# Two layers of a hybrid mixer with feed-forward sublayers: the last feed-forward sublayer partly by seven products instead of eight

## The chip, the cores and the metric

The kernel runs on one core of one Trainium2 chip. The metric is the device time of one execution in microseconds (us). The profile is one execution recorded by the hardware profiler. Its names for the engines: PE is TensorE (the matmuls), PEld TensorE's weight loads, DVE is VectorE, ACT is ScalarE, POOL is GpSimd and SP is SyncE, whose queue issues the DMAs.

## The reference, cut to what matters

Two layers run over 512 tokens of width 1024 and 256 context tokens. Each layer has a feed-forward sublayer, a mixer and a second feed-forward sublayer. In the last layer the second feed-forward sublayer is needed for the 512 tokens alone, and it ends the program.

```python
def swiglu(h, wg, wu, wd):
    return (jax.nn.silu(h @ wg) * (h @ wu)) @ wd
...
        x = residual(x, 0.5 * swiglu(sublayer_in(x, m_l, 2), ffn_w_gate[l, 1], ffn_w_up[l, 1], ffn_w_down[l, 1]),
                     m_l, 2, norm_g[l, 2], norm_b[l, 2])
```

`wg` and `wu` are 1024 x 2816, `wd` is 2816 x 1024, all in float32.

## The kernel before

Every float32 operand of a product is held as two float16 pieces, a rounded one and its remainder, and a product is made of three passes (large x large, large x small, small x large). `split_weight` (L319) makes the pieces of a weight: ScalarE scales and rounds (L320), VectorE subtracts (L321). Activations are split in the same way (L457, L458).

The 2816 columns of the feed-forward sublayer are 11 pairs of 256 columns, and the pairs form five groups (`GROUPS`, L355: 0-1, 2-3, 4-5, 6-7, 8-10). For each pair, gate and up are computed, the silu and the product follow, and `put_act` (L441) makes the activation's pieces. After each group its down product is added to the accumulator `acc`. The last group's down (`down_last`, L803) ends in the normalisation.

Both products can be made in two ways.

- Plain. `gate_up_plain` (L557) makes 96 products of 512 columns a pair in the 512-token sublayer (L571), in the PSUM tiles `big`. `down_plain` (L762) makes 96 products for a group of two (L772), in the PSUM tiles `sm`. A pair's gate and up need 8 weight pieces (`ring` blocks), a pair's down 4.
- By seven. A block product of 2 x 2 halves is made of seven products instead of eight (Winograd's form of Strassen's scheme). `gate_up` (L488) splits the tokens and the 1024 inputs into halves, so that a pair takes 168 products, each over half of the tokens (L511), in the PSUM tiles `pf` (one running chain for each of gate and up) and `big`; ScalarE copies the chain at three points (L518), and VectorE adds (L534, L544, L546). `down_blocks` (L722) makes the seven products of a group (L743), two token tiles at a time, in `pf` and `big`, and VectorE adds them to the accumulator (L749). The weights need sums of their quarters, which GpSimd makes (L426 to L429 for gate and up, L394 to L397 for down), and 7 pieces for each of gate, up and down. The activations need four more sums (L449 to L452) and 7 pieces instead of 4. The inputs need four differences (`tt`, made by `differences`, L463) over the whole sublayer: `input_differences` (L478) loads the scaled inputs `inp` that the sublayer before wrote to memory (L299 to L301, only where `keep` is set) and forms them on VectorE and GpSimd.

In the three sublayers of 768 tokens (`has_ctx`), pair 0 is plain, the other ten go by seven, and so do the downs of the first four groups. In the last sublayer (`whole_plain`) all pairs and groups are plain, and the inputs' differences are not made.

Weights come in loads of 1 MB into two `raw` tiles. `jobs` lists the loads and splits in the order of use, and `prepare` (L838) runs three of them ahead; the pieces stand in 21 ring blocks, five of which lie in the sublayer's own memory and can be written only after the mixer's memory is free. The differences and the copies of the chain share the tiles `pt` with the rows that the residual loads (L796). The accumulator shares the tiles `xa` with the loaded inputs. The order of the instructions on each engine is set by the tile framework's scheduler, which mixes instructions of different steps by priority and by its own estimate of time.

Of the kernel before, what the change touches and what calls it, by code (L numbers as in the profile page):

```python
# [23 lines left out]
DEPTH = 2  # L24
FF = 2816
NPAIR = FF // 256
# [17 lines left out]
def kernel(  # L44
# [25 lines left out]
    class Tags:  # L70


        def __init__(self, pool, **bufs):
            self.pool, self.bufs = pool, bufs
# [124 lines left out]
    def affine_cols(l, i, prev):  # L199

        cols = small.tile([P, 2, KC, 2], F32, tag="abc", name=f"abc{l}{i}", bufs=2)
        sc1 = small.tile([P, KC, 2], F32, tag="sc1", name=f"sc1{l}{i}", bufs=2)
        V.tensor_scalar(out=sc1, in0=mT[l][:, 3 * i + 1], scalar1=1.0, scalar2=SA, op0=ALU.add, op1=ALU.mult)
        g = gb_cols[:, 0, prev, :].unsqueeze(2).to_broadcast([P, KC, 2])
        b = gb_cols[:, 1, prev, :].unsqueeze(2).to_broadcast([P, KC, 2])
        V.tensor_tensor(out=cols[:, 0], in0=sc1, in1=g, op=ALU.mult)
        V.tensor_tensor(out=sc1, in0=sc1, in1=b, op=ALU.mult)
        V.scalar_tensor_tensor(out=cols[:, 1], in0=mT[l][:, 3 * i], scalar=SA, in1=sc1,
                               op0=ALU.mult, op1=ALU.add)
        return cols  # L210
# [25 lines left out]
    def bcast_row(src, nm, alloc):  # L236
        t = alloc([P, D], nm)
        nc.sync.dma_start(out=t, in_=src.partition_broadcast(P))
        return t
# [10 lines left out]
    class Norm:  # L250


        def __init__(self, l, i, nxt, last, arow, ayh, au32):
            self.l, self.i, self.last, self.ayh, self.au32 = l, i, last, ayh, au32
            self.st = {}
            n = 3 * l + i
            rows = (norm_g[l, i], norm_b[l, i]) if last else (agb[n], agb[6 + n])
            self.g, self.b = (bcast_row(q, f"{nm}{l}{i}", arow) for q, nm in zip(rows, ("gbc", "bbc")))
            if not last:
                self.uT = new_uT(f"uT{l}{i}")  # L260
                self.cols = affine_cols(nxt[0], nxt[1], 3 * l + i)
                self.stream = Stream((l, i))
                self.keep = nxt[1] != 1 and nxt != (DEPTH - 1, 2)

        def one(self, t, rt):

# [42 lines left out]
    def new_uT(nm):  # L309
        return main.tile([P, 2, KC, T], F16, tag="uT", name=nm, bufs=1)  # L310
# [44 lines left out]
    GROUPS = [[0, 1], [2, 3], [4, 5], [6, 7], [8, 9, 10]]  # L355

    def ffn(l, i, uT, stream, ntiles, nxt, last, todo):
        has_ctx = ntiles > NLT
# [4 lines left out]
        with tc.tile_pool(name=f"ffn{l}{i}", bufs=1) as fp:  # L363
# [14 lines left out]
                return block(shape, nm)  # L378


            whole_plain = not has_ctx
            gu_plain = set(range(NPAIR)) if whole_plain else {0}
            plain = set(range(NPAIR)) if whole_plain else set(GROUPS[-1])

            def prep_down(pr_):
                raw = load_raw(ffn_w_down[l, w, pr_ * 256:(pr_ + 1) * 256, :].rearrange("(k p) f -> p k f", p=P),
# [20 lines left out]
            def load_plain(pr_):  # L407
                for q in range(2):
                    load(pr_, q)
# [64 lines left out]
            def new_differences():  # L474
                for n in range(1, 5):
                    tt[n] = ft("T", [P, 2, 4, half], f"T{n}{l}{i}", F16)

            def input_differences():  # L478
                new_differences()
                for t in range(ntiles // 2):  # L480
                    u = []
                    for q in range(2):
                        u.append(ft("xa", [P, KC, P], f"u{l}{i}{t}{q}"))
                        nc.sync.dma_start(out=u[q], in_=stream.inputs[t + q * ntiles // 2])
                    differences(u[0][:, 0:4], u[1][:, 0:4], u[0][:, 4:8], u[1][:, 4:8], slice(0, 4),
                                slice(t * P, (t + 1) * P), [P, 4, P], f"{t}")
# [231 lines left out]
            def new_acc():  # L718
                for t in range(ntiles):
                    acc[t] = ft("xa", [P, D], f"acc{l}{i}_{t}")  # L720
# [123 lines left out]
            if start:  # L844
                finish = first_pair()
            else:
                load_plain(0)
                if not whole_plain:
                    input_differences()
            prepare(FIT)  # L850
            for gi, prs in enumerate(GROUPS):
                for q in prs:
                    if todo and (q > 1 or len(todo) >= NPAIR - 1 - q):
                        ada_vec(*todo.pop(0), al("ada"))
                    if start and q == 0:
                        finish()
                    else:
                        (gate_up_plain if q in gu_plain else gate_up)(q)
                    if q == 0:
                        new_acc()  # L860
                    ahead[0] -= 2 if q > 0 else 0
                    prepare(FIT)
                    if gi == len(GROUPS) - 1 and q < NPAIR - 1:
                        residual(q - prs[0])
                if gi < len(GROUPS) - 1:
                    (down_plain if whole_plain else down_blocks)(gi, prs)
                    ahead[0] -= 2
                    prepare(FIT)
            norm = down_last(GROUPS[-1])
# [765 lines left out]
    for n, (l, i) in enumerate(steps):  # L1635
        last = n == len(steps) - 1
        nxt = None if last else steps[n + 1]
# [70 lines left out]
```

## Time and profile before

| | |
|---|---|
| time, median of 3 runs | 2877.5 us (2873.37 to 2879.3) |
| profiled execution | 2878.8 us |
| its span | 2877.0 us |
| TensorE busy | 2656.4 us, 92% |
| VectorE busy | 2118.9 us, 74% |
| ScalarE busy | 1210.6 us, 42% |
| GpSimd busy | 1160.1 us, 40% |
| mean granted clock of TensorE | 0.973 |

The last sublayer's first product starts at 2511.95 us and its last one ends at 2868.06 us. Times in the rows are counted from the span's start. In a row of the timeline, the start and the length come first, then engine, line, operation, tiles and shapes; xN is the number of instructions merged, and the brackets give the idle time of the engine before it and what ended that. Instructions overlap in the pipeline, so the pitch of a run of N products is the difference of two starts divided by N.

### The profile page before, as it was taken

What the parts mean: (1) busy time and instruction counts of PE and PEld (TensorE: products, weight loads), DVE (VectorE), ACT (ScalarE), POOL (GpSimd) and SP (SyncE); (2) the same over time, 40 slices, a digit from 0 to 9 for tenths busy, and PEclk for the clock granted to TensorE, in tenths of its full rate; (3) what the DMA queues carried; (4) which work ended last, traced back from release to release, by engine and by line L of the source; (5) the groups of instructions that cost most, each with busy time, mean ns of one, the idle gap of its engine ahead of it and who ended that gap; (6) DMA issues with size and microseconds to landing.
All of it is one profiled execution on the core that took longest, in us unless ns stands there. A gap on an engine that the chain in (4) does not pass through costs nothing. (4 is left out here: it accounts for less than half of the span.)

```text
span 2877.0 us, 42905 instructions
## 1 busy us (share of the span) xinstructions
PE 2656.4 (92%) x16415; PEld 1554.0 (54%) x16415; DVE 2118.9 (74%) x3134; ACT 1210.6 (42%) x2619; POOL 1160.1 (40%) x1016
## 2 busy tenths in 40 slices
PE   6899999989899988999999889988999899899998
PEld 4454555557677863544555444544555667744443
DVE  4967788786867688768877988879787768634455
ACT  3443344434436444533443344433433537333321
POOL 1744465241525455534552655446242425400011
PEclk8999999999999999999999999999999999999999
DMA  7635432333234244444453422221422333152330
GB/s 242 196 127 176 133 132 98 107 121 90 78 88 105 74 176 163 160 161 147 147 169 121 165 65 82 74 66 61 156 83 87 103 107 100 67 176 88 120 122 30
DMA packets 220355, 342.63 MB, mean 119 GB/s; under 512 B 16008, under 2 KB 162166, under 8 KB 220150
## 3 DMA queue, kind: packets, MB, share of 16 engines
q1 hardware_dynamic: 220150, 339.90, 36.6%
q8 instruction: 129, 2.11, 0.3%
q14 instruction: 76, 0.62, 0.1%
HBM read 301.43 MB, written 23.22 MB: 113 GB/s over the span
## 5 line engine op out<-in xcount | busy, mean ns | idle before, releaser
L511 PEld LDWEIGHTS <-pcgu 128*128 128x128 f16 x3792 | 373.4, 99 | 329.1 <-issue 93.3
L511 PE MATMUL ch<-T,pcgu 128*128 128x384 f16 x1920 | 337.0, 329 | 5.2 <-ACT U L518 5.2
L743 PEld LDWEIGHTS <-act 128*128 128x128 f16 x1512 | 142.9, 98 | 216.4 <-issue 58.4
L321 DVE SCALAR_TENSOR_TENSOR pcgu<-rawgu,pcgu 128x512 f16<-128x512 f32 x218 | 216.3, 1008 | 49.2 <-ACT pcgu L320 48.2
L571 PE MATMUL pl<-uT,pcgu 128*128 128x512 f16 (+2 forms) x1068 | 228.0, 367 | 7.7 <-DVE uT L214 7.0
L320 ACT ACTIVATE pcgu<-rawgu 128x512 f16<-128x512 f32 x218 | 133.9, 626 | 211.5 <-PE ds L743 126.6
L429 POOL TENSOR_TENSOR S4gu<-rawgu,S2gu 128x512 f32<-128x512 f32 x60 | 90.1, 1502 | 273.7 <-DVE pcgu L321 137.3
L571 PEld LDWEIGHTS <-pcgu 128*128 128x128 f16 x1236 | 121.8, 101 | 138.5 <-issue 24.7
L511 PEld LDWEIGHTS <-pegu 128*128 128x128 f16 x1248 | 122.2, 98 | 108.2 <-issue 29.7
L800 POOL TENSOR_TENSOR acc<-acc,gate 128x512 f32<-128x512 f32 x44 | 62.2, 1421 | 282.9 <-DVE acc L780 253.7
L743 PE MATMUL ds<-pcd,act 128*128 128x512 f16 x612 | 152.3, 381 | 4.3 <-DVE acc L749 2.8
L743 PE MATMUL dc<-pcd,act 128*128 128x512 f16 x576 | 149.1, 384 | 7.2 <-DVE acc L749 7.1
L976 PEld LDWEIGHTS <-uT 128*128 128x128 f16 x1344 | 134.7, 101 | 29.9 <-issue 8.4
L228 ACT ACTIVATE u<-pt,abc 128x128 f32<-128x128 f32 x224 | 81.2, 467 | 161.2 <-PE pt L225 98.9
L816 PE MATMUL pd<-pcd,act 128*128 128x512 f16 x594 | 141.1, 379 | 4.2 <-DVE dt L822 4.2
L321 DVE SCALAR_TENSOR_TENSOR pcd<-rawd,pcd 128x512 f16<-128x512 f32 x124 | 109.0, 893 | 40.6 <-ACT pcd L320 40.5
L426 POOL TENSOR_TENSOR S1gu<-rawgu 128x512 f32<-128x512 f32 x60 | 88.8, 1480 | 116.2 <-DMA rawgu<-in_ffn_w_gate_dram 55.8
L816 PEld LDWEIGHTS <-act 128*128 128x128 f16 x792 | 77.4, 98 | 99.2 <-issue 10.7
L458 DVE TENSOR_TENSOR act<-sg,act 128x384 f16<-128x384 f32 (+1 forms) x149 | 123.6, 873 | 3.3 <-ACT act L457 3.3
L94 POOL TENSOR_SCALAR rs<-mv 128x1 f32<-128x1 f32 x32 | 17.9, 559 | 263.3 <-DVE mv L273 263.3
L518 ACT COPY U<-ch 128x384 f32<-128x384 f32 x180 | 83.6, 472 | 76.8 <-PE ch L511 76.1
L428 POOL TENSOR_TENSOR S3gu<-rawgu 128x512 f32<-128x512 f32 x60 | 96.4, 1607 | 32.4 <-DVE pegu L321 16.2
(391 smaller groups left out, 6209.5 us busy)
## 6 DMA issues: line engine op xcount, KB each, us to landing
adaw<-in_ada_w_dram SPq DMA_DIRECT2D x128, 512.0 KB
rawd<-in_ffn_w_down_dram SPq DMA_DIRECT2D x44, 1024.0 KB
rawgu<-in_ffn_w_gate_dram SPq DMA_DIRECT2D x43, 1024.0 KB
rawgu<-in_ffn_w_up_dram SPq DMA_DIRECT2D x43, 1024.0 KB
row<-yh SPq DMA_DIRECT2D x56, 256.0 KB
rawwo<-in_w_out_dram SPq DMA_DIRECT2D x8, 1024.0 KB
xt<-row SPq DMA_DIRECT2D x32, 256.0 KB
gate<-grow SPq DMA_DIRECT2D x28, 256.0 KB
```

The lines of the kernel that those rows point to most:

```text
L320: A.activation(pc[:, 0], src, AF.Copy, scale=SW)
L321: V.scalar_tensor_tensor(out=pc[:, 1], in0=src, scalar=SW, in1=pc[:, 0], op0=ALU.mult, op1=ALU.subtract)
L426: G.tensor_tensor(out=s1, in0=a21, in1=a22, op=ALU.add)
L428: G.tensor_tensor(out=s3, in0=a11, in1=a21, op=ALU.subtract)
L429: G.tensor_tensor(out=s4, in0=a12, in1=s2, op=ALU.subtract)
L458: V.tensor_tensor(out=pc[:, 1], in0=src, in1=pc[:, 0], op=ALU.subtract)
L511: PE.matmul(pp, lhsT=wt[pr_][q][m][:, a, k, :], rhs=rhs, start=(n == 0 and m in (1, 2, 5)), stop=(n == 11), skip_group_check=m in (1, 6, 7 ...
L518: A.copy(t_, chain[q])
L571: PE.matmul(pp[:, j, o:o + hi - lo], lhsT=wp.at(a, k, cc * P, (cc + 1) * P), rhs=uT[:, b, k, lo:hi], start=(n == 0), stop=(n == KC * 3 - 1))
L743: PE.matmul(pd, lhsT=acts[q][m][:, a, ts], rhs=wd[q][m][:, b], start=(n == 0 and m in (1, 2, 5)), stop=(n == len(prs) * 3 - 1), skip_group ...
L816: PE.matmul(pd, lhsT=acts[q][2 * cc + hf][:, a, o:o + P], rhs=wd[q][2 * cc + h][:, b], start=(n == 0), stop=(n == len(prs) * 6 - 1))
L976: PE.matmul(pp, lhsT=uT[:, a, k, t * P:(t + 1) * P], rhs=pc.at(b, k, 0, n_), start=(n == 0), stop=(n == KC * 3 - 1))
```

## The change

In the last sublayer the gate and up of the odd pairs (1, 3, 5, 7, 9) go by seven products, and so do the downs of groups 1 and 3 (pairs 2, 3 and 6, 7). The even pairs and the groups 0, 2 and 4 stay plain. The mixer of the last layer now writes the scaled inputs to memory (`keep`), and the sublayer loads them and forms their differences after pair 0. The 768-token sublayers stay as they are.

```diff
-                self.keep = nxt[1] != 1 and nxt != (DEPTH - 1, 2)
+                self.keep = nxt[1] != 1
...
-            whole_plain = not has_ctx
-            gu_plain = set(range(NPAIR)) if whole_plain else {0}
-            plain = set(range(NPAIR)) if whole_plain else set(GROUPS[-1])
+            gu_plain = {0} if has_ctx else set(range(0, NPAIR, 2))
+            plain = set(GROUPS[-1] + ([] if has_ctx else GROUPS[0] + GROUPS[2]))
...
                 load_plain(0)
-                if not whole_plain:
+                if has_ctx:
                     input_differences()
...
                     if q == 0:
+                        if not has_ctx:
+                            input_differences()
                         new_acc()
...
-                    (down_plain if whole_plain else down_blocks)(gi, prs)
+                    (down_plain if prs[0] in plain else down_blocks)(gi, prs)
```

## Rows read from the trace of the kernel before

**Rows 1.** The page: busy time, share of the span and instructions of each engine, and the lines of the chain that ended last.

```profile
PE 2656.4 (92%) x16415; PEld 1554.0 (54%) x16415; DVE 2118.9 (74%) x3134; ACT 1210.6 (42%) x2619; POOL 1160.1 (40%) x1016
...
PE pl L571 7%; PE pd L772 3%; PE pd L816 1%; DMA rawd<-in_ffn_w_down_dram 0%; DMA rawgu<-in_ffn_w_gate_dram 0%; DVE pcgu L321 0%; POOL yh L306 0%; POOL yh L305 0%; DMA row<-yh 0%; ACT pcd L320 0%; POOL rs L94 0%; DVE bst L271 0%; DVE pegu L321 0%; ACT L437 0%; DVE yh L286 0%
```

**Rows 2.** Busy time of each engine in two stretches of the last sublayer: start, end and length, busy us and instructions of each engine, TensorE's granted clock, the DMA engines' share and GB/s.

```profile
2529.00:2546.70 17.70, 16.04 (x144) 11.03 (x145) 6.98 (x11) 6.90 (x12) 0.00 (x0) 0.84 0.95 340
2546.70:2868.10 321.40, 321.32 (x1488) 145.44 (x1487) 147.39 (x243) 96.49 (x185) 16.48 (x14) 1.00 0.30 98
```

**Rows 3.** Who TensorE waited for from 2546.7 to 2868.1 us (us in total, times, longest).

```profile
PE pl L571 <- DVE sg L438: 1.5, 1, 1.5
```

**Rows 4.** Timeline of TensorE at the start of pair 1, products of 512 columns.

```profile
2546.72 1.46 PE L571 MATMUL pl<-uT,pegu 128*128 128x512 f16 x6 [1.51 <-DVE sg L438]
2548.01 4.05 PE L571 MATMUL pl<-uT,pcgu 128*128 128x512 f16 x18
2551.90 1.46 PE L571 MATMUL pl<-uT,pegu 128*128 128x512 f16 x6
```

**Rows 5.** Timeline of TensorE in the last mixer's output projection, products of 256 columns.

```profile
2458.19 18.61 PE L1566 MATMUL pm<-pcwo,mT 128*128 128x256 f16 x169
2476.64 1.04 PE L225 MATMUL pt<-mats,yh 128*128 128x128 f32 x8
```

**Rows 6.** Groups of instructions from 2546.7 to 2868 us (count, then busy us and mean ns of one, then idle time before them and what ended it).

```profile
L571 PEld LDWEIGHTS <-pcgu 128*128 128x128 f16 x732 | 71.6, 98 | 86.4
...
L321 DVE SCALAR_TENSOR_TENSOR pcgu<-rawgu,pcgu 128x512 f16<-128x512 f32 x55 | 38.0, 708 | 20.7 <-ACT pcgu L320 20.4
...
L458 DVE TENSOR_TENSOR act<-sg,act 128x256 f16<-128x256 f32 x44 | 16.6, 420 | 3.3 <-ACT act L457 3.3
```

**Rows 7.** Timeline of VectorE near 2543 us: three weight subtractions, and three activation pieces.

```profile
2543.12 1.89 DVE L321 SCALAR_TENSOR_TENSOR pcd<-rawd,pcd 128x512 f16<-128x512 f32 x3
...
2548.80 1.10 DVE L458 TENSOR_TENSOR act<-sg,act 128x256 f16<-128x256 f32 x3 [0.47 <-ACT act L457]
```

**Rows 8.** The line of GpSimd's first weight sum, over the whole span: durations in ns (least, median, most), first and last start.

```profile
L426 POOL TENSOR_TENSOR S1gu<-rawgu x60: 1262/1598/1721, 58.5 to 2035.2; 128x512 f32<-128x512 f32 x60
```

**Rows 9.** Timeline of SP's queue at the start of the last sublayer.

```profile
2508.77 17.71 SPq L307 DMA_DIRECT2D row<-yh  x4
2528.42 0.32 SPq L786 DMA_DIRECT2D gate<-grow  x1
2528.80 1.37 SPq L796 DMA_DIRECT2D xt<-row  x3
2530.21 0.43 SPq L337 DMA_DIRECT2D rawgu<-in_ffn_w_up_dram  x1
```

**Rows 10.** Timeline of all engines at the start of the 768-token sublayer after the first mixer: the loads of the inputs, and the first and last instruction of the differences on VectorE.

```profile
1057.38 3.57 SPq L484 DMA_DIRECT2D u<-inp  x6
...
1063.47 0.69 DVE L466 TENSOR_TENSOR t<-u,u 128x512 f32<-128x512 f32 x1 [3.51 <-DMA u<-inp]
...
1084.48 1.28 DVE L472 TENSOR_TENSOR T<-t,T 128x512 f16<-128x512 f32 x2
```

**Rows 11.** Timeline of TensorE in pair 1 of the same sublayer, the rows with a wait.

```profile
1079.30 1.46 PE L511 MATMUL ch<-uT,pegu 128*128 128x384 f16 x8 [1.36 <-DVE sg L438]
...
1086.41 2.11 PE L511 MATMUL sd<-uT,pegu 128*128 128x384 f16 x12 [1.70 <-ACT sg L437]
...
1093.56 1.12 PE L511 MATMUL ch<-uT,pcgu 128*128 128x384 f16 x3 [4.71 <-DVE sg L438]
...
1107.15 1.35 PE L511 MATMUL sd<-T,pegu 128*128 128x384 f16 x6 [3.99 <-DVE sg L534]
```

**Rows 12.** Timeline of TensorE in pair 1 of the second layer's 768-token sublayer, the rows with the three long waits.

```profile
1651.83 2.11 PE L511 MATMUL sd<-uT,pegu 128*128 128x384 f16 x12 [3.04 <-ACT sg L437]
...
1658.98 4.00 PE L511 MATMUL ch<-uT,pcgu 128*128 128x384 f16 x12 [3.74 <-DVE sg L438]
...
1672.54 4.00 PE L511 MATMUL sd<-T,pegu 128*128 128x384 f16 x12 [3.57 <-DVE sg L534]
```

**Rows 13.** Busy time of each engine in one cycle of two pairs and a down of the same sublayer, and in 4.2 us of it (columns as in rows 2).

```profile
1785.80:1878.56 92.76, 84.75 (x463) 45.49 (x463) 75.72 (x96) 39.11 (x74) 45.03 (x33) 0.98 0.22 69
1825.00:1829.20 4.20, 3.60 (x12) 1.66 (x12) 2.42 (x4) 1.62 (x4) 2.73 (x3) 0.62 0.01 3
```

**Rows 14.** Who TensorE waited for in that cycle, the four largest (us in total, times, longest).

```profile
PE dc L743 <- DVE acc L749: 3.1, 2, 2.8
PE ch L511 <- DVE acc L749: 2.8, 1, 2.8
PE sd L511 <- DVE up L534: 0.8, 1, 0.8
PE ch L511 <- ACT U L518: 0.6, 1, 0.6
```

**Rows 15.** Timeline of TensorE in that cycle: 12 products after a wait, and 12 without one.

```profile
1825.10 3.60 PE L511 MATMUL ch<-uT,pcgu 128*128 128x384 f16 x12 [2.83 <-DVE acc L749]
...
1832.83 2.11 PE L511 MATMUL sd<-T,pcgu 128*128 128x384 f16 x12
```

**Rows 16.** Groups of instructions in that cycle (columns as in rows 6): the largest group of weight subtractions, and of activation pieces.

```profile
L321 DVE SCALAR_TENSOR_TENSOR pcgu<-rawgu,pcgu 128x512 f16<-128x512 f32 x9 | 10.5, 1176 | 1.0 <-ACT pcgu L320 1.0
L458 DVE TENSOR_TENSOR act<-sg,act 128x384 f16<-128x384 f32 x7 | 9.8, 1448 | 0.0
```

## The prediction

> **What bounds the kernel now.** The page first: TensorE is busy 92% of the span, and the chain that ended last names L571, the gate/up products of the plain pairs, more than any other line [rows 1]. Then the busy time by stretches: from 2546.7 to 2868.1 us, the last sublayer after its first pair, TensorE is busy 321.3 of 321.4 us at full granted clock, VectorE 147 us and GpSimd 16 us [rows 2]. The list of waits has one entry there, 1.5 us at its start [rows 3]. So each TensorE microsecond saved there is one of the time, until another engine takes its place, and each wait that the change brings costs at once.
>
> **What a product costs.** 24 products of 512 columns start from 2546.72 to 2551.90: 215.8 ns each [rows 4]. For 256 columns, which the change uses, the nearest rows are the mixer's output products, 169 with a new weight each from 2458.19 to 2476.64: 109.2 ns [rows 5]. A weight load takes 98 ns [rows 6] and fits beside. Against this stands the Trainium skill, "TensorE: Matmul & The Clock Gate", section "Back-to-back issue gap": a sustained stream of loads and products at about 81 ns for 128 columns and 131 ns for 512. By an estimate between these, 98 ns for 256 columns, seven products would cost a pair 16.4 us against 12.6, so 3.8 us more. The 215.8 ns measured at 512 differ from the page, and the rows decide.
>
> **What goes.** Gate/up of a pair: 2 matrices x 2 column halves x 8 k x 3 passes = 96 products x 215.8 ns = 20.72 us. By seven: 7 x 2 matrices x 4 k x 3 passes = 168 of 256 columns x 109.2 ns = 18.35 us. Saved 2.37 us, in five pairs (1, 3, 5, 7, 9) 11.9 us. Down of a group of two: 96 products become 7 x 2 tiles x 2 pairs x 3 = 84, still of 512 columns: 12 x 215.8 ns = 2.59 us, in two groups (pairs 2, 3 and 6, 7) 5.2 us. Together **17.1 us**, all on the path.
>
> **What comes on the other engines.** Seven products need 14 weight pieces for 8 (five pairs) and 7 for 4 (four down matrices): 30 + 12 = 42 more splits, each a ScalarE scale and a VectorE subtraction. Three of these take 1.89 us, one 0.69, so they issue every 0.60 us; activation pieces (three in 1.10, one 0.42) every 0.34 [rows 7, 6]. 42 x 0.60 = 25 us. GpSimd makes 5 x 8 + 4 x 4 = 56 weight sums, of which one takes 1.26 us at least and 1.60 in the median [rows 8]: 71 to 90 us, and 16 smaller sums of activations. There are 12 more activation pieces and 28 accumulator additions instead of 16. Over 321 us no engine is full: VectorE goes from 147 to some 200 us. So I cost them at nothing, hidden by TensorE; the cover is gone where they bunch, and that is a rival below.
>
> The four writes of the scaled inputs (512 KB each) enter SP's queue at the mixer's end, among row writes and weight loads; SP stands in row writes from 2508.8 to 2526.5 anyway [rows 9], so zero. The loads of the residual's rows, issued as early as 2528.8 now [rows 9], come later, because the differences and copies take their buffers (pt); the last group needs them, with two pairs' products over them: zero, about 2 us if one were met bare. Two of the four accumulator tiles wait until the inputs' tiles are released, and are first written after pair 1: zero.
>
> **The first pairs.** By its third product pair 1 now needs the differences. Their loads can start when the mixer's memory is free, about 2528.4 us, as the next loads do now [rows 9]; the DMA engines are 95% busy from 2529 to 2546.7 [rows 2], but the residual's rows leave room. After the first mixer, 768 tokens, the same loads are issued at 1057.4, the first difference starts at 1063.5 and the last ends at 1085.8 [rows 10]: 6.1 us, then 22.3 us for three column tiles, so about 15 for two: ready near 2549.5. TensorE reaches them at about 2545.2 + 48 x 109.2 ns = 2550.4. Just in time. Yet in both 768-token sublayers TensorE stalls in pair 1, with ScalarE and VectorE, in order, busy with differences and splits: 11.8 us in four waits after the first mixer [rows 11], 10.4 in the second layer (3.0, 3.7, 3.6), and there two runs of 12 products took 4.00 us, not 2.11 [rows 12]. The 4.7 and 3.7 are for the PSUM of the 256 context tokens, not used here, and the 1.5 us of [rows 3] falls away, because pair 1 can begin in another PSUM tile. Bounds: -1.5 us, and 14 ([rows 12] with the slow products). I take 5: a wait of 3.6 us, which both have, about 2 for the silu, 1 for the clock, less 1.5.
>
> **The other pairs.** The nearest rows are a cycle of two pairs and a down in the second layer's 768-token sublayer, 92.8 us [rows 13]; the second pair of the group has only the 0.8 us for an addition out of PSUM [rows 14], the first one up to 2.8. Pairs 3, 5, 7, 9 stand second or inside a group; 256 columns leave a third less slack than 384. So 0 to 2.8 us each; I take 0.8, four times: 3.1.
>
> **The groups by seven.** Now the down's PSUM tiles (sm) are its own, and the next pair's gate/up fills every wait. By seven it takes pf and big, which that pair needs too. In the cycle of [rows 14] the down waits 3.1 us (2.8 at once) for accumulator additions, queued on VectorE behind activation pieces, which queue behind GpSimd's sums. The pair after it waited 2.8 us for pf and ran 12 products in 3.60 us, not 2.11 [rows 15], at a granted clock of 0.62 [rows 13], so partly at 1.2 GHz; here a plain pair follows, which takes big, released earlier. From 0 to 7.3 us a group (all of [rows 14]); I take 3.1 twice: 6.2.
>
> **Sum.** -17.1 + 5 + 3.1 + 6.2 = **-2.8 us**. The profiled execution took 2878.8 us, 1.8 more than its span of 2877.0, and is 1.3 above the median of 2877.5. Against the median I forecast **2874.5 us**, a saving mostly paid back, with a range of its own of 2867 to 2882.
>
> **Rivals.** (1) *Covered.* The waits are filled: pairs 0.4, groups 1.0, the start 0: -17.1 + 1.6 + 2 = -13.5, **2864**. For it: VectorE is under half busy now, and second pairs have few waits. Against: the down of the cycle waited [rows 14].
>
> (2) *VectorE full in groups 1 and 3*, the slower side. In one of them (plain pair, seven pair, down by seven: TensorE 20.7 + 18.4 + 18.1 = 57.2 us) VectorE has 36 splits, 14 activation pieces, 14 accumulator additions of 0.60 us and about 4.5 us more. Alone, 36 x 0.60 + 14 x 0.34 + 12.9 = 39 us. But with GpSimd at work the largest groups of splits and pieces take 1.18 and 1.45 us in the mean [rows 16], against 0.71 and 0.42 in the last sublayer now [rows 6]; VectorE is busy 75.7 of 92.8 us there [rows 13]. It decides once splits average over 0.96 us (pieces at 0.7, an estimate between 0.42 and 1.45): 36 x 0.96 + 9.8 + 12.9 = 57.3. At 1.18 it is 65.2, 8 over, twice 16 in place of the 6.2: -17.1 + 16 + 5 + 1.6 (pairs 5, 9) = +5.5, and with half the group waits on top +8.6: **2886**. Against it: 13 of the 36 splits may slip into the plain group that follows. The Trainium skill, "SBUF — State Buffer", section "Who interferes with whom", says that a VectorE instruction with two SBUF inputs and a GpSimd one that reads SBUF exclude each other for their whole length. The rows agree in kind; an estimate by that rule locks 36 x 0.60 + 14 x 0.34 + 16 x 1.26 + 8 x (0.65 to 1.26) = 52 to 57 of the 57 us: just full, no more.
>
> (3) *A late start.* The upper bound of the first pairs, 14 for 5: **2883.5**. The order on ScalarE and GpSimd decides.
>
> (4) *Short products not at half.* If weight loads set the pace and a 256-column product takes 123 ns, the pairs gain nothing: -2.8 + 11.9, **2886.5**. 169 products at 109.2 ns speak against it. The page cited first points that way.
>
> **Chances.** Forecast 0.48, covered 0.22, VectorE full 0.17, late start 0.09, short products 0.04. A measurement here can tell about 0.2%, 5.8 us, from no change: faster is below 2871.7, slower above 2883.3. The forecast's own range gives 0.15 faster, 0.29 same, 0.04 slower; covered is faster; the late start 0.05 same, 0.04 slower; VectorE full slower; short products 0.01 same, 0.03 slower. Faster 0.37, same 0.35, slower 0.28. From 2862 to 2888 leaves out a quarter of covered and half of VectorE full, some 0.15.
>
> **What would show it.** Right: 840 L511 products of 256 columns at 109 ns and 168 of L743 in this sublayer, TensorE's busy time there down by 17 us, and some 14 us of waits: at pair 1, and two near 3 us for L749. Covered: hardly a wait after 2560. VectorE full: its share over 95% from pair 2 to the end of group 1, splits over 1 us. Late start: waits on L471 or L472. The forecast is wrong if the groups' waits are elsewhere, or if the end's sequence changes.

## The result, and the profile after

The changed kernel takes 2900.9 us (median of 4 runs, 2897.0 to 2908.8), the kernel before beside it 2875.4 (2869.6 to 2879.3): a ratio of 1.0094, 95% interval 1.0065 to 1.0123. It is 25 us slower. The forecast was 2874.5, its range 2862 to 2888.

The profiled execution has a span of 2896.9 us. The last sublayer's first product starts at 2508.1 us, where it was 2511.95 before. From there to the end of the span it is 388.8 us against 365.05: **+23.7 us**. So nearly all of the loss lies in the changed sublayer, and this measure is given for every run below, because the work ahead of the sublayer, which the edits leave as it is but for the four writes of the inputs, varies by some microseconds from one execution to the next: in the fourteen profiled executions the first product starts between 2503.4 and 2516.1 us.

The page after, the lines that answer to [rows 1]:

```profile
PE 2641.0 (91%) x16751; PEld 1583.0 (55%) x16751; DVE 2234.2 (77%) x3247; ACT 1254.6 (43%) x2716; POOL 1268.3 (44%) x1092
...
PE pl L570 3%; PE pd L771 1%; PE pd L815 1%; DVE pcgu L321 1%; PE ch L510 1%; DVE pcd L321 1%; DVE act L457 1%; PE sd L510 1%; PE dc L742 1%; DMA rawgu<-in_ffn_w_up_dram 0%; DMA rawgu<-in_ffn_w_gate_dram 0%; DVE ped L321 0%; DVE T L471 0%; 
```

In the changed kernel the lines of the sublayer stand one lower: L510 is the product of `gate_up`, L570 of `gate_up_plain`, L742 of `down_blocks`, L748 its addition to the accumulator, L437 the product behind the silu, L457 the activation's pieces. TensorE's busy time fell by 15.4 us, as wanted, and the time rose: the chain that ended last now runs through VectorE's splits (L321) and pieces (L457) as well.

Timeline of TensorE in pair 5, of the changed kernel (answers to [rows 5]):

```profile
2683.77 2.78 PE L510 MATMUL ch<-uT,pcgu 128*128 128x256 f16 x24
2686.39 1.47 PE L510 MATMUL sd<-uT,pegu 128*128 128x256 f16 x12
2687.70 1.47 PE L510 MATMUL sd<-uT,pcgu 128*128 128x256 f16 x12
```

24 products in 2.62 us: 109.2 ns each, the price that the prediction took, and no gap. Pairs 5 and 9 lose nothing.

Busy time of each engine in stretches of the changed kernel (columns as in [rows 2]): pair 2, plain; pair 3 and the down of group 1, both by seven; pair 4 and pair 5 with 12 products of the next down between; and the first 4.9 us after the longest wait of that down.

```profile
2593.50:2614.20 20.70, 20.70 (x98) 9.35 (x97) 12.60 (x14) 10.94 (x20) 7.22 (x5) 1.00 0.28 101
2614.20:2663.10 48.90, 38.76 (x250) 24.74 (x249) 46.35 (x65) 25.10 (x53) 25.29 (x20) 0.93 0.32 104
2663.10:2706.00 42.90, 42.90 (x284) 27.53 (x283) 26.24 (x41) 19.80 (x39) 8.08 (x6) 1.00 0.40 128
...
2648.00:2652.90 4.90, 4.84 (x13) 1.72 (x13) 3.90 (x9) 0.93 (x3) 1.15 (x1) 0.57 0.20 67
```

The second row is the loss. Its products are worth 168 x 109.2 ns + 84 x 215.8 ns = 36.5 us, and it takes 48.9: 12.4 us are lost in group 1. VectorE is busy 46.35 of the 48.9 us, 95%, and that is 10 us more than the products last, so TensorE can't run ahead of it. In the row before, VectorE has 8 us idle. Pair 7 with the down of group 3 takes 52.6 us (2743.55 to 2796.18): 16.1 us are lost there. The last row shows what follows a wait: the granted clock is 0.57 of full speed, so mostly at the lower level of 1.2 GHz, and the 12 products that start from 2648.06 to 2652.69 take 4.63 us instead of 2.59.

Who TensorE waited for from 2540 to 2900 us in the changed kernel, the five largest entries (answers to [rows 3], where 1.5 us stood):

```profile
PE dc L742 <- DVE acc L748: 11.8, 2, 6.5
PE sd L510 <- DVE sg L533: 6.1, 2, 3.3
PE sd L510 <- DVE sg L437: 4.6, 3, 2.2
PE ch L510 <- DVE pcgu L321: 1.8, 2, 1.4
PE pl L570 <- DVE sg L543: 1.6, 1, 1.6
```

All five name VectorE. The 11.8 us are one wait in each down by seven (5.2 and 6.5), the 6.1 one in each of pairs 3 and 7. The 4.6 are 2.2 in pair 1 and 1.2 in each of pairs 3 and 7.

Groups of VectorE's instructions in the stretch of pair 3 and the down (columns as in [rows 6]):

```profile
L321 DVE SCALAR_TENSOR_TENSOR pcgu<-rawgu,pcgu 128x512 f16<-128x512 f32 x10 | 8.4, 843 | 1.3 <-ACT pcgu L320 1.3
L457 DVE TENSOR_TENSOR act<-sg,act 128x256 f16<-128x256 f32 x5 | 5.6, 1162 | 0.0
L321 DVE SCALAR_TENSOR_TENSOR pcd<-rawd,pcd 128x512 f16<-128x512 f32 x4 | 4.8, 1211 | 0.0
L457 DVE TENSOR_TENSOR act<-up,act 128x256 f16<-128x256 f32 x8 | 4.7, 611 | 0.0
L321 DVE SCALAR_TENSOR_TENSOR ped<-B,ped 128x512 f16<-128x512 f32 x3 | 4.5, 1514 | 0.0
...
L748 DVE TENSOR_TENSOR acc<-acc,ds 128x512 f32<-128x512 f32 x6 | 3.9, 674 | 0.0
```

The groups of splits shown take 0.84 to 1.51 us in the mean, where [rows 6] had 0.71; all 30 splits of the stretch, with those not shown, 0.97. The pieces take 1.16 us, those of the activation's sums 0.61, where [rows 6] had 0.42. The addition L748, which reads one operand from PSUM, takes 0.67.

Timeline of VectorE, GpSimd and TensorE ahead of the 5.2 us wait, changed kernel:

```profile
2642.89 0.90 POOL L449 TENSOR_TENSOR up<-up,sg 128x256 f32<-128x256 f32 x1
2643.13 1.21 DVE L321 SCALAR_TENSOR_TENSOR pcgu<-rawgu,pcgu 128x512 f16<-128x512 f32 x1
2643.75 1.71 POOL L426 TENSOR_TENSOR S2gu<-S1gu,rawgu 128x512 f32<-128x512 f32 x1
...
2644.26 1.48 DVE L457 TENSOR_TENSOR act<-up,act 128x256 f16<-128x256 f32 x1
2645.42 1.44 POOL L427 TENSOR_TENSOR S3gu<-rawgu 128x512 f32<-128x512 f32 x1
...
2645.66 1.75 DVE L321 SCALAR_TENSOR_TENSOR pcgu<-rawgu,pcgu 128x512 f16<-128x512 f32 x1
...
2647.33 1.27 DVE L748 TENSOR_TENSOR acc<-acc,dc 128x512 f32<-128x512 f32 x2
2648.06 1.44 PE L742 MATMUL dc<-pcd,act 128*128 128x512 f16 x3 [5.24 <-DVE acc L748]
...
2650.40 0.68 DVE L321 SCALAR_TENSOR_TENSOR pcgu<-S2gu,pcgu 128x512 f16<-128x512 f32 x1
2651.00 0.68 DVE L321 SCALAR_TENSOR_TENSOR pcgu<-S3gu,pcgu 128x512 f16<-128x512 f32 x1
```

Read it from the wait upwards. The down needs a PSUM tile that L748 empties. L748 is short, but stands on VectorE behind two splits of a later pair's weights and a piece for this down. They take 1.21, 1.48 and 1.75 us, and each ends 0.3 to 0.6 us after a GpSimd sum beside it has ended (at 2643.79, 2645.46 and 2646.86). At 2650.4, with GpSimd idle, two splits take 0.68 each.

### The profile page after: what moved, and what is told of

The parts are those of the page before. It is cut to its first block, busy times and chain, and to the rows that moved or that the text cites. A ratio compares the mean times of both kernels' runs of the same rounds, so it can differ in the third digit from the quotient of the medians.

```text
span 2896.9 us, 43976 instructions
## 1 busy us (share of the span) xinstructions
PE 2641.0 (91%) x16751; PEld 1583.0 (55%) x16751; DVE 2234.2 (77%) x3247; ACT 1254.6 (43%) x2716; POOL 1268.3 (44%) x1092
## 5 line engine op out<-in xcount | busy, mean ns | idle before, releaser
L510 PEld LDWEIGHTS <-pcgu 128*128 128x128 f16 x4428 | 434.9, 99 | 350.1 <-issue 101.7
L510 PE MATMUL ch<-T,pcgu 128*128 128x384 f16 (+1 forms) x2208 | 372.7, 322 | 8.3 <-ACT U L517 8.2
L742 PEld LDWEIGHTS <-act 128*128 128x128 f16 x1680 | 160.2, 99 | 253.5 <-issue 77.7
L321 DVE SCALAR_TENSOR_TENSOR pcgu<-rawgu,pcgu 128x512 f16<-128x512 f32 x210 | 221.9, 1070 | 48.9 <-ACT pcgu L320 47.6
L428 POOL TENSOR_TENSOR S4gu<-rawgu,S2gu 128x512 f32<-128x512 f32 x70 | 106.2, 1517 | 308.5 <-DVE pcgu L321 171.9
L510 PEld LDWEIGHTS <-pegu 128*128 128x128 f16 x1452 | 142.2, 98 | 110.5 <-issue 29.3
L742 PE MATMUL dc<-pcd,act 128*128 128x512 f16 x648 | 168.9, 386 | 12.7 <-DVE acc L748 12.5
L742 PE MATMUL ds<-pcd,act 128*128 128x512 f16 x672 | 167.6, 380 | 5.0 <-DVE acc L748 2.8
L570 PE MATMUL pl<-uT,pcgu 128*128 128x512 f16 (+2 forms) x696 | 143.5, 360 | 8.7 <-DVE uT L214 6.0
L977 PEld LDWEIGHTS <-uT 128*128 128x128 f16 x1344 | 132.8, 99 | 28.5 <-issue 8.9
L321 DVE SCALAR_TENSOR_TENSOR pcd<-rawd,pcd 128x512 f16<-128x512 f32 x122 | 113.0, 934 | 32.2 <-ACT pcd L320 32.0
L570 PEld LDWEIGHTS <-pcgu 128*128 128x128 f16 x864 | 84.2, 101 | 94.6 <-issue 26.0
L457 DVE TENSOR_TENSOR act<-sg,act 128x384 f16<-128x384 f32 (+1 forms) x145 | 132.4, 956 | 1.4 <-ACT act L456 1.4
L815 PEld LDWEIGHTS <-act 128*128 128x128 f16 x792 | 77.5, 98 | 99.6 <-issue 11.5
L517 ACT COPY U<-ch 128x384 f32<-128x384 f32 (+1 forms) x210 | 94.7, 457 | 81.4 <-PE ch L510 80.2
L510 PE MATMUL sd<-uT,pcgu 128*128 128x384 f16 (+1 forms) x684 | 114.7, 316 | 5.5 <-DVE sg L437 3.4
```

The lines of the kernel that those rows point to most:

```text
L321: V.scalar_tensor_tensor(out=pc[:, 1], in0=src, scalar=SW, in1=pc[:, 0], op0=ALU.mult, op1=ALU.subtract)
L428: G.tensor_tensor(out=s4, in0=a12, in1=s2, op=ALU.subtract)
L457: V.tensor_tensor(out=pc[:, 1], in0=src, in1=pc[:, 0], op=ALU.subtract)
L510: PE.matmul(pp, lhsT=wt[pr_][q][m][:, a, k, :], rhs=rhs, start=(n == 0 and m in (1, 2, 5)), stop=(n == 11), skip_group_check=m in (1, 6, 7 ...
L517: A.copy(t_, chain[q])
L570: PE.matmul(pp[:, j, o:o + hi - lo], lhsT=wp.at(a, k, cc * P, (cc + 1) * P), rhs=uT[:, b, k, lo:hi], start=(n == 0), stop=(n == KC * 3 - 1))
```

## The experiments

**Theory A**: GpSimd's weight sums and VectorE's splits exclude each other in time; so where a pair by seven, a down by seven and the preparation of such weights meet, VectorE has more to do than TensorE. **Rivals**: B, the down by seven loses by its PSUM tiles alone; C, the start of the sublayer (the differences) costs most; D, VectorE has too many instructions, whoever makes the sums. Each ratio is against runs of the kernel before taken beside that run, whose medians run from 2873.4 to 2877.0 us, so medians of different rows don't compare to 0.1%. The last column is the time from the sublayer's first product to the end of the span, in one profiled execution, less the 365.05 us of the kernel before.

| run | by seven in the last sublayer | ratio (95%) | median us | sublayer |
|---|---|---|---|---|
| the change | gate/up 1, 3, 5, 7, 9; downs 1, 3 | 1.0094 (1.0065 to 1.0123) | 2900.9 | +23.7 |
| e1 | gate/up alone | 1.0013 (1.0002 to 1.0024) | 2879.1 | +3.0 |
| e2 | downs alone | 0.9993 (0.9983 to 1.0003) | 2870.1 | -3.9 |
| e3 | the change without weight sums | 0.9989 (0.9980 to 0.9999) | 2871.3 | -7.2 |
| e4 | gate/up 3, 5, 7, 9 | 0.9997 (0.9987 to 1.0008) | 2873.9 | -1.8 |
| e5 | e4, differences after pair 1 | 0.9995 (0.9982 to 1.0008) | 2873.6 | -3.4 |
| e6 | gate/up 5, 9; downs 1, 3 | 1.0052 (1.0038 to 1.0067) | 2886.6 | +11.7 |
| e7 | nothing; unused weight sums | 1.0054 (1.0040 to 1.0067) | 2888.3 | +7.9 |
| e8 | gate/up 2 to 10 | 1.0032 (1.0020 to 1.0044) | 2880.6 | +6.6 |
| e9 | e4, differences after pair 2 | 0.9993 (0.9982 to 1.0005) | 2873.9 | -1.8 |
| e10 | the change, weight sums on VectorE | 1.0030 (1.0017 to 1.0043) | 2886.1 | +8.2 |
| e11 | e10 without pair 1, differences after pair 2 | 1.0066 (1.0046 to 1.0085) | 2896.5 | +17.6 |
| e12 | downs 0 to 3 | 1.0009 (0.9998 to 1.0020) | 2877.7 | -1.0 |

**Each part alone: e1, e2.** The diffs are against the changed kernel. In e1 all downs are plain:

```diff
-            plain = set(GROUPS[-1] + ([] if has_ctx else GROUPS[0] + GROUPS[2]))
+            plain = set(GROUPS[-1]) if has_ctx else set(range(NPAIR))
```

In e2 all gate/up are plain, and the differences are left out (the inputs are still written):

```diff
-            gu_plain = {0} if has_ctx else set(range(0, NPAIR, 2))
+            gu_plain = {0} if has_ctx else set(range(NPAIR))
...
-                        if not has_ctx:
-                            input_differences()
```

> The odd pairs' gate/up stay by seven, all downs are plain again. Theory A (VectorE, slowed by GpSimd's sums, is full in groups 1 and 3, and everything queued on it is late): pairs 3 and 7 become like pairs 5 and 9, which lost nothing; all 28.5 us lost from pair 3 to the end of down 1 and from pair 7 to the end of down 3 go away, and with them the 5.2 us saved by the downs; pair 1's start keeps its loss of about 8: 2875.4 - 11.9 + 8 = 2872 us. VectorE's busy share from pair 3 to pair 4 falls from 95% to under 80%. Theory B (the down by seven waits because its PSUM tiles are those of the next pair, so nothing fills its gaps; the gate/up waits of pairs 3 and 7 are their own): only the downs' waits and slow products go (17 us), the waits on L533 and L437 in pairs 3 and 7 stay: 2883 us.

> The downs of groups 1 and 3 stay by seven, all gate/up is plain, no differences of the inputs are made. Theory A: VectorE has 30 splits in such a group instead of 36, GpSimd 8 weight sums instead of 16, the queue drains, the wait before the sixth product's start (L748) falls from 5.2 and 6.5 us to 2 or less: 2875.4 - 5.2 + 4 = 2874 us. Theory B: the waits of 5 to 6 us and the slow products behind them stay, about 7 us a group: 2875.4 - 5.2 + 15 = 2885 us.

Waits of TensorE in e2 from 2540 to 2860 us:

```profile
PE ds L742 <- DVE acc L748: 2.0, 2, 1.0
PE dc L742 <- DVE acc L748: 0.3, 1, 0.3
```

A down by seven alone waits about 1 us, not 5 to 6: rival B is out. In e1 TensorE loses 4.2 us after 2580 us, where the change loses 28.5 in its two groups, and pairs 3 and 7 have no wait over 0.3 us. Its time lies between theory A's 2872 and rival B's 2883 all the same: of the 14.9 us that it loses (11.9 + 3.0), 10.7 lie ahead of 2580 us, where 8 were expected. The parts give +3.0 and -3.9 us; together they give +23.7. So 24.6 us belong to neither part, but to both at once.

**The weight sums: e3, e7, e10.** e3 leaves out the weight sums of the last sublayer (the pieces are split from the quarters as they are); the number of splits, pieces and products is that of the change. e7 is the kernel before, with the change's 56 weight sums made and used by nobody. e10 makes the 56 sums on VectorE. Of each, the edit for gate and up is shown; the down's t1 to t4 are treated likewise. e3:

```diff
+                if has_ctx:
                     G.tensor_tensor(out=s1, in0=a21, in1=a22, op=ALU.add)
...
+                else:
+                    s1, s2, s3, s4 = a21, a11, a21, a12
```

e7, against the kernel before:

```diff
+                    if whole_plain and pr_ % 2:
...
+                        G.tensor_tensor(out=s1, in0=a21, in1=a22, op=ALU.add)
...
```

e10:

```diff
+                E = G if has_ctx else V
-                G.tensor_tensor(out=s1, in0=a21, in1=a22, op=ALU.add)
+                E.tensor_tensor(out=s1, in0=a21, in1=a22, op=ALU.add)
```

> The changed kernel, but in the last sublayer GpSimd's weight sums (8 for each odd pair's gate and up, 4 for each down by seven) are left out; the pieces that should hold sums are split from quarters of the weights, so part of the computation is left out. VectorE's and ScalarE's instructions, all products, all PSUM tiles stay. Theory A in the form that GpSimd's sums slow VectorE: splits fall from over 1 us back to 0.7, the waits on L748 to 2 or less, the groups' 28.5 us of loss to about 8: about 2875 us. Theory B, or VectorE full by the count of its instructions alone: little changes, 2893 to 2900 us, waits of 5 us stay.

> The kernel before, with the weight sums of the change made on GpSimd (five pairs' gate/up, two groups' down) and used by nobody; products, splits and everything else are as before. It shows what GpSimd's sums cost VectorE's splits by themselves. If the two exclude each other (theory A): the mean of a split rises from 0.71 us towards 1.0 to 1.2 us in the stretches with sums, at an unchanged number of them, and the time stays within 0.2%, because VectorE isn't full with the splits of plain pairs alone. If GpSimd's sums hurt only because the splits have to wait for their results: a split stays at 0.7 us.

> The change as it is, but in the last sublayer the 56 weight sums are made on VectorE (0.68 us each, by the differences on that engine) instead of GpSimd. If the loss is that GpSimd's sums make the splits longer (theory A): splits fall back to about 0.7 us, and a group by seven asks VectorE for 36 x 0.68 + 16 x 0.68 + 14 x 0.55 + 14 x 0.68 + 4 = 56.6 of 57.2 us, full but no longer over by 14: 2 to 5 us are lost a group, ratio 1.002 at most, 2868 to 2880. If VectorE is simply overloaded by what it has to do, whoever makes the sums: it now has 38 us more, and the kernel is slower than the change, 2905 or more.

Pair 3 and the down of group 1 in e3 (busy time, then VectorE's largest group):

```profile
2608.70:2647.50 38.80, 35.46 (x241) 23.41 (x240) 36.41 (x63) 23.13 (x50) 7.43 (x8) 1.00 0.41 136
...
L321 DVE SCALAR_TENSOR_TENSOR pcgu<-rawgu,pcgu 128x512 f16<-128x512 f32 x15 | 10.6, 715 | 1.7 <-ACT pcgu L320 1.7
```

The same in e10:

```profile
2612.90:2658.30 45.40, 39.12 (x241) 24.00 (x240) 41.17 (x74) 23.12 (x49) 9.70 (x8) 0.92 0.36 117
...
L321 DVE SCALAR_TENSOR_TENSOR pcgu<-rawgu,pcgu 128x512 f16<-128x512 f32 x10 | 6.8, 684 | 1.5 <-ACT pcgu L320 1.5
```

The down's wait in e3 (L756 there is the addition to the accumulator):

```profile
PE dc L750 <- DVE acc L756: 6.7, 2, 3.3
```

And e7 from 2560 to 2868 us (busy time, then groups of VectorE; L472 there is the line of the activation's pieces):

```profile
2560.00:2868.00 308.00, 308.00 (x1426) 139.54 (x1425) 162.75 (x222) 93.91 (x178) 80.95 (x59) 1.00 0.28 93
...
L321 DVE SCALAR_TENSOR_TENSOR pcgu<-rawgu,pcgu 128x512 f16<-128x512 f32 x55 | 43.7, 816 | 19.0 <-ACT pcgu L320 18.8
L472 DVE TENSOR_TENSOR act<-sg,act 128x256 f16<-128x256 f32 x40 | 31.2, 819 | 3.3 <-ACT act L471 3.3
L321 DVE SCALAR_TENSOR_TENSOR pcd<-rawd,pcd 128x512 f16<-128x512 f32 x30 | 25.6, 881 | 12.3 <-ACT pcd L320 8.4 <-PE pl L585 3.9
```

In e3 the same stretch takes 38.8 us instead of 48.9 (0.9 of it because eight more products of pair 3 had run ahead of it), with 63 VectorE instructions for 65: 36.4 us of work for 46.4. The whole sublayer is 30.9 us faster than with the sums. But the downs still wait 3.3 us each for the addition, not 2 or less as expected, and in the two groups some 9 of the 28.5 us are still lost: even with the sums for nothing, the sublayer would keep 7.2 of the 17.1 us.

In e7 nothing waits for the sums, and still the pieces go from 0.42 to 0.82 us, the largest group of splits from 0.71 to 0.82 and the down's splits from 0.69 (in the kernel before, from 2560 to 2856 us) to 0.88; VectorE is busy 162.8 us, where the kernel before has 139.5 in the same 308. So the splits don't grow by a dependence on the sums, they grow by the sums' running at the same time. (The 1.0 to 1.2 us expected were for stretches with sums; these means are over all 308 us.) After 2560 us e7 loses nothing, as theory A expects, since VectorE has room. But the time, expected within 0.2%, is 0.54% up; that is the price of its start, told below, which wasn't expected.

In e10 the splits are back at 0.68 us, and the stretch takes 45.4 us in place of 48.9, and the sublayer 15.5 us less than in the change, though VectorE has 56 instructions more. With more instructions less is lost, and in e3 their number is that of the change: that speaks against rival D, a count of instructions. But e10 ends at 2886, past the 2868 to 2880 expected: VectorE still has 41.2 us of work for 36.5 us of products, and of the 28.5 us in the two groups e10 loses some 20 (its second group takes 46.1 us). So the sums cost on VectorE too, only less than on GpSimd.

The Trainium skill, "SBUF — State Buffer", section "Who interferes with whom", states the rule: a VectorE instruction with two SBUF inputs and a GpSimd one that reads SBUF exclude each other, one being blocked until the other has ended, while a VectorE instruction with at most one SBUF input, outside its two-port modes, is left alone. The rows agree on both sides: splits and pieces grow (0.97 and up to 1.16 us in the mean), L748, with one operand in PSUM, does not (674 ns).

**In time, not in the group: e6.** The seven pairs 5 and 9 stand in other groups than the downs by seven.

```diff
-            gu_plain = {0} if has_ctx else set(range(0, NPAIR, 2))
+            gu_plain = {0} if has_ctx else set(range(NPAIR)) - {5, 9}
...
+                    if q == 1 and not has_ctx:
+                        input_differences()
```

> Gate/up by seven only in pairs 5 and 9, down by seven in groups 1 and 3, whose own pairs are all plain; differences after pair 1. Saved at most 2 x 2.37 + 2 x 2.59 = 9.9 us. If the loss needs the weight sums of a seven pair and of a down by seven within one group (theory A, a load on VectorE and GpSimd that is local): waits stay as in e2 and e1, about 2 us: ratio 0.997, about 2866. If the kernel loses wherever both kinds stand in the sublayer, by what they hold in common (ring blocks, tiles of the differences, PSUM): half of the loss of both together stays, 12 us, and the ratio is 1.001 or more, 2877 or more.

Busy time in e6 in the down of group 3:

```profile
2766.50:2793.90 27.40, 20.91 (x83) 8.38 (x82) 27.40 (x32) 8.67 (x17) 21.62 (x17) 0.88 0.25 77
```

The expectation was wrong: +11.7 us, in the range that it gave to things held in common (2877 or more). But a wait for those would show as idle time, and VectorE is busy in all 27.4 us and GpSimd in 21.6, for a down worth 84 x 215.8 ns = 18.1 us, though pairs 6 and 7 are plain. The timeline has the reason: the sums S1gu to S4gu and splits there are pair 9's, because `prepare` runs three loads ahead. The price depends on which preparation falls into the down's time, two pairs on, not on the group. In e2, where none of it does, the downs wait 1.0 and 1.3 us.

**The start: e4, e5, e9.** e4 takes pair 1 out; e5 and e9 ask for the differences later. In all three the downs are plain, as in e1, and

```diff
-            gu_plain = {0} if has_ctx else set(range(0, NPAIR, 2))
+            gu_plain = {0} if has_ctx else {0, 1, 2, 4, 6, 8, 10}
```

In e5, and in e9 with `q == 2`:

```diff
-                        if not has_ctx:
-                            input_differences()
...
+                    if q == 1 and not has_ctx:
+                        input_differences()
```

> Gate/up by seven in pairs 3, 5, 7, 9 only, all downs plain; pair 1 is plain, so the differences have one plain pair and a down more. If pair 1's loss of about 8 us is the haste of the start (differences, splits of 14 pieces and the silu of pair 0 at once), it goes: 2875.4 - 9.5 + 0 to 2 = 2867 us, and no wait over 1 us before 2860. If the first pair by seven pays wherever it stands, pair 3 has the loss: 2874 us.

> Gate/up by seven in pairs 3, 5, 7 and 9, all downs plain, and the inputs' differences made after pair 1 instead of pair 0, so that no product needs them before pair 3. If the 5.1 us wait of e4 at 2550 us is the silu and pieces of pair 0 queued behind the differences (theory A): that wait goes, and 4 x 2.37 = 9.5 us are kept less at most 1 us of new waits: ratio 0.997, about 2866. If the differences cost TensorE the same wherever they stand: the wait turns up at pair 2, ratio 0.999 to 1.000, 2870 to 2874.

> As e5 (gate/up by seven in pairs 3, 5, 7, 9, all downs plain), with the inputs' differences one pair later still, after pair 2. In e5 the wait of 5.7 us before pair 1 stayed, since VectorE took up the differences at 2530 to 2548 us all the same, ahead of the splits and of pair 0's silu. If that is the cause: the work is asked for later, the wait falls to the 1.5 us of the kernel before, and 9.5 us less at most 1 us are kept: ratio 0.997, about 2865. If the scheduler pulls the differences forward again, the wait stays at 5 us: ratio 0.999, about 2870.

Waits of TensorE in e4, in e5 and in e9, a fence each, the entries of 1 us or more behind pair 0:

```profile
PE pl L570 <- DVE sg L437: 5.1, 1, 5.1
```

```profile
PE pl L570 <- DVE sg L437: 5.7, 1, 5.7
```

```profile
PE sd L510 <- DVE sg L437: 2.6, 1, 2.6
PE pl L570 <- DVE sg L437: 2.0, 1, 2.0
PE ch L510 <- DVE T L471: 1.0, 1, 1.0
PE pd L771 <- DVE act L457: 1.0, 1, 1.0
```

In e4 pair 3 loses nothing, but the plain pair 1 waits 5.1 us for pair 0's silu product, which stands behind the differences on VectorE: its 2873.9 us is that of the expectation's other case (2874) by chance, not by its mechanism. In e5 the 5 us wait did not go: VectorE still took the differences from 2534 to 2548 us, ahead of pair 0's silu product. In e9 it shrank to 2.0, and 4.6 us of new waits came at pair 3 (2607.8 to 2614.1), among them one for the differences themselves. So asking later moved the price, it did not remove it, and both miss the 2865 and 2866 expected. Four pairs by seven save 9.5 us, and 1.8 to 3.4 of it are left.

**Looking for a better version: e8, e11, e12.** e8 has nine pairs by seven, all downs plain as in e1, and the differences where e5 has them. e11 puts the edits of e4 (its first line), e9 and e10 together. e12 is the kernel before with four downs by seven. The lines of e8 and, against the kernel before, of e12:

```diff
-            gu_plain = {0} if has_ctx else set(range(0, NPAIR, 2))
+            gu_plain = {0} if has_ctx else {0, 1}
```

```diff
-            plain = set(range(NPAIR)) if whole_plain else set(GROUPS[-1])
+            plain = set(GROUPS[-1])
...
-                    (down_plain if whole_plain else down_blocks)(gi, prs)
+                    down_blocks(gi, prs)
```

> Gate/up by seven in pairs 2 to 10 (nine pairs), all downs plain, differences after pair 1. Groups 1 to 3 now have 28 + 8 = 36 splits and 16 weight sums in 57.4 us of products, as many splits as groups 1 and 3 of the change, but 4 sums fewer of activations a pair, 8 pieces instead of 14 and 8 additions to the accumulator instead of 14, and no down that waits for them. Saved at most 9 x 2.37 = 21.3 us. If splits and weight sums alone fill VectorE (theory A in its narrow form): 10 us or more are lost in each of three groups, and the ratio is 1.003 or more, 2883 or more. If it takes the extra work of a down by seven as well (theory A in its wide form): VectorE is at 80 to 90%, losses of 1 to 3 us a group, ratio 0.995, 2858 to 2864.

> Pairs 3, 5, 7, 9 and groups 1 and 3 by seven, the differences after pair 2, and the weight sums on VectorE: what the two runs above would be together. Saved at most 9.5 + 5.2 = 14.7 us. With 2 to 5 us lost in each of the two groups and 1 us at the start (theory A): ratio 0.996 to 0.999, 2862 to 2871. If VectorE is overloaded by the sums wherever they are made: 2880 or more.

> All gate/up plain, no differences and no inputs kept, and the downs of groups 0 to 3 by seven: the one part that cost little (e2, where two such downs kept 3.9 of 5.2 us of the sublayer). Saved at most 4 x 2.59 = 10.4 us. If a down by seven alone leaves VectorE room (theory A; in e2 it was busy 27 of 40 us around one), each keeps about 1.9 us: ratio 0.997, 2866 to 2869. If four in a row fill VectorE and GpSimd, because the weight sums now come in every group: 3 us or more are lost in each, ratio 1.000 to 1.002.

Waits in e8 from 2560 to 2870 us, the three largest entries:

```profile
PE ch L510 <- ACT U L517: 7.8, 7, 2.5
PE pd L771 <- ACT act L456: 2.1, 2, 1.5
PE sd L510 <- DVE up L545: 1.7, 1, 1.7
```

Timeline of e12 at the end of pair 0:

```profile
2538.28 1.76 DVE L321 SCALAR_TENSOR_TENSOR pcd<-rawd,pcd 128x512 f16<-128x512 f32 x1
2539.44 1.71 POOL L396 TENSOR_TENSOR B<-rawd 128x512 f32<-128x512 f32 x1
...
2541.85 1.58 POOL L397 TENSOR_TENSOR B<-rawd,B 128x512 f32<-128x512 f32 x1 [0.69 <-DVE pcd L321]
2542.23 1.74 DVE L321 SCALAR_TENSOR_TENSOR ped<-B,ped 128x512 f16<-128x512 f32 x1
...
2543.89 0.68 DVE L438 SCALAR_TENSOR_TENSOR sg<-pl,sg 128x512 f32<-128x512 f32 x1
2544.63 1.87 PE L571 MATMUL pl<-uT,pegu 128*128 128x512 f16 x4 [5.05 <-DVE sg L438]
```

e8 would save 21.3 us and ends 6.6 above: adjoining pairs by seven, with no down by seven, lose in many small waits for ScalarE's copies and for VectorE. TensorE idles 2.1, 1.7 and 3.4 us in the three stretches of 60 us from 2563 us on, and 10.4 from 2743 to 2863. So no group loses the 10 us of the narrow form; the ratio is that form's because the start (a wait of 5.2 us) and the last pairs lose as well.

e11 fell furthest from its expectation (2862 to 2871), into the range given to rival D: its differences, after pair 2, meet group 1, where TensorE waits 6.4 us for them, and both downs still wait 4 us for the addition to the accumulator.

In e12 the downs wait 0.5 to 1.3 us each, as expected, but the first product of pair 1 waits 5.05 us, with no differences at all: here the sums of group 0's down lengthen the splits ahead of pair 0's silu product L438. e7's unused sums did the like: waits of 8.2 and 3.8 us at 2537 and 2556, where the kernel before has 5.3 and 1.5. Its sublayer takes 7.9 us more and its first product waits 2.2 us longer, 10 of e7's 15 us; the other 5 are not explained. None of the versions that compute the whole result is faster than the kernel before by more than its interval.

## Why the prediction was wrong

- **What bounds the kernel, what a product costs, what goes**: right. 109.2 ns at 256 columns; TensorE's busy time fell by 15.4 us, about the 17.1 less what products after waits took longer. The rival of short products not at half is refuted.
- **What comes on the other engines, costed at nothing**: this cover failed. It was read over 321 us, in which VectorE would rise to some 200; but the time is lost in stretches of 49 us where it was 95% busy.
- **The other pairs, 0.8 each**: 0 in pairs 5 and 9. Pairs 3 and 7 have waits of 5 us each (4.9 and 4.8 of the waits over 0.3 us), but by the neighbouring down: in e1 they have none.
- **The groups by seven, 3.1 each**: this is the step that failed. Its place was right, one long wait in each down for the addition to the accumulator; its size wasn't. With pairs 3 and 7 the prediction had 2 x (3.1 + 0.8) = 7.8 us; measured were 12.4 + 16.1 = 28.5. The waits taken from [rows 14] were those of a cycle with 768 tokens, in which VectorE is busy 75.7 of 92.8 us [rows 13]. With 512 tokens the products last two thirds as long, but the weights to be split and summed are as many. VectorE's work, which fitted under the products there, doesn't here: 46.4 us against 36.5.
- **VectorE full, 2886 at 0.17**: the right mechanism at half its price. It spread VectorE's work over 57.2 us, a plain pair included. In fact VectorE idled 8 us in the plain pair, and 46.4 us of work stood against 36.5 us of products behind it. The two groups lost 28.5 us, not 16. Its deciding point, splits over 0.96 us in the mean, was just reached: the 30 splits took 0.97 us in group 1's stretch and 1.02 in group 3's. By its sum, over 57.2 us, that is a loss of 2 us at most; over the shorter stretch it is the loss measured.
- **The first pairs, 5**: mis-sized. From 2544.1 to 2575.3 us the changed kernel loses 10.3 us, where 1.5 stood before, and the wait at 2528.8 grew from 5.3 to 7.6: 11 in all. That is near the size of the late start (14), but not its sign: no wait in the changed kernel is for the differences (L471). e12 loses about 5 us there without differences, and what is late there is mostly VectorE's work, splits and silu products. So rival C is a part of the loss, not the most of it.

A slip besides: 2877.5 less 2.8 is 2874.7, not 2874.5. The sum by measured terms: -17.1 + 11 + 28.5 + 0.6 for a wait in `down_last` = 23.0, against 23.7.

What stays open: in e10 the splits are short again, and 10 us a group remain; in e3, without any sums, some 9 in both together. Whether they need less work or only another order on VectorE, L748 first, was not tried.

## What to carry to other kernels

Before you trade TensorE time for VectorE and GpSimd work, make the balance for the shortest stretch in which the new work meets, not for the stage; leave room in it for VectorE instructions that grow beside GpSimd, those with both inputs in SBUF (in e7, 64 us more of GpSimd made VectorE busy 23 us longer). When rows come from the same code at a larger size, scale the terms apart: products shrink with the tokens, the preparation of the weights doesn't. Two edits that are each within 0.15% of no change alone (1.0013, 0.9993) made it 0.9% slower together, so their sum is no forecast where they share an engine.

## What the runs showed that was not expected

- GpSimd's sums cost VectorE without any dependence: 64 us more of GpSimd in e7 (81.0 against 16.5 in [rows 2], over a slightly shorter stretch) took the activation's pieces from 0.42 to 0.82 us. The additions out of PSUM took 0.68, as before.
- A wait on TensorE can cost more than its length: after the 5.2 us wait 12 products took 4.63 us for 2.59, at a granted clock of 0.57. It doesn't always: after e3's two waits of 3.3 us in the downs, 12 products took 2.59 us one time and 4.27 the other.
- The start of the sublayer has no slack on VectorE: the differences (e4, e5) and the sums of one down (e12) each make TensorE wait 5 to 5.7 us in the same place, where 1.5 stood. Moved later (e9), the differences still make 5 us of waits more, 2.0 + 4.6 for 1.5.
